# Down projection of a decoder layer: four chunks of features, the middle two by seven block products

## The chip, the cores and the metric

The kernel runs on one core of a Trainium2 chip. A core has a matrix engine (TensorE, PE in the profile; its weight loads are PEld), a vector engine (VectorE, DVE), a scalar engine (ScalarE, ACT), GpSimd (POOL) and SyncE (SP), which issues most transfers. Work lies in SBUF (128 partitions), matmuls accumulate in banks of PSUM, and transfers between device memory and SBUF go through 16 DMA engines. The metric is device time in microseconds (us) of one execution of the whole program.

## The reference, cut to what matters

One layer of a hybrid decoder over 576 tokens (512 of a prompt, 64 of samples), width 1024: a mixer, a cross attention, and at the end a gated feed-forward with 2816 hidden features. The change lies in the last part:

```python
u = _rms(x) * g_pre_ffn
f = (jax.nn.silu(u @ w_gate) * (u @ w_up)) @ w_down
x = x + _rms(f) * g_post_ffn
```

## The kernel before

All large products are made in split form. A float32 operand is kept as a high part (rounded to the matmul type `float32r`) and a low part (the remainder), and a product takes three matmuls: high by high, high by low, low by high. So every weight that is loaded must be split: ACT casts the high part (`whi`), and the low part (`wlo`, `wacc`) is made by a subtraction on DVE, or by ACT writing the negated high part and a POOL transfer accumulating the weight onto it (`accum_op=ALU.add`).

The 2816 hidden features are 22 blocks of 128; gate and up weights have one unit of 1024 columns per feature block (8 blocks of inputs by 128). Tokens are 576 columns, in halves of 288 (`EHALVES`) or of 256 and 320 (`HALVES`).

Feature blocks 0 to 3 are made plainly, in a stretch whose order is written out by hand: `at_(p, ...)` puts each step at a place p of a plan, and the plan is issued in that order. Blocks 4 to 21 are made by the class `Pair` (L1659). It takes two neighbouring feature blocks j and j+1 as a 2 by 2 grid: inputs in two halves, tokens in two halves. Seven products of blocks take the place of eight (Winograd's form of Strassen's scheme). The weights' sums and differences are made on DVE in `sums` and `diffs`, and split in `parts2`, `parts3` and `parts4`; the sums of the token blocks were made once. One unit (the gate, or the up weights of one pair of blocks) has 7 products of 4 x 3 matmuls of 288 columns, 84 in all. `prepare` issues the preparation of a unit. Its matmuls come in three parts: `early` (products 0 and 1), `mid` (2, 3, 4) and `late` (5, 6), and `pairs` issues early, the previous unit's late, then mid. `done` (L1734) takes a result from PSUM: the gate passes through silu into the tile `gt`, the up product is multiplied onto it, and the hidden block is split into `hh` and `hl`.

The down projection is cut into three chunks of feature blocks: 0 to 7, 8 to 15 and 16 to 21 (the loop at L1846, and L1853 onward). In a chunk, `down_chunk` (L1794) makes all 8 output blocks in both halves, with 24 matmuls in the first two chunks (18 in the last) for each. Chunk 0 copies the results into the tile `f2` (`ev_first`, ACT), chunk 1 adds to it (`ev_add`, DVE), and the last chunk adds and goes on to the norm. Pairs 4 and 6 come before chunk 0, pairs 8 to 14 before chunk 1, pairs 16 to 20 before the last one.

What sets the order: outside the hand-written stretches a planner reorders the instructions of each engine before the run, by its own estimate of when operands and buffers are ready; on the chip each engine works through its queue in the order given. Buffers come from small rings: raw weights `raw` (2) and `rawx` (2), `whi` (3), `wlo` (3), `wacc` (2), and three PSUM banks for each of two sides. A load on SP waits for its raw buffer, and all later loads of SP wait behind it.

Of the kernel before, what the change touches and what calls it, by code (L numbers as in the profile page):

```python
# [11 lines left out]
F32 = mybir.dt.float32  # L12
# [3 lines left out]
ALU = mybir.AluOpType  # L16
# [100 lines left out]
def build(nc, tc, ctx, I, O):  # L117
# [912 lines left out]

    ph = ctx.enter_context(tc.tile_pool(name="rows", bufs=1, reuse_waits="tile"))
    spb.close()
# [386 lines left out]

    u3h = SL(3, "u3h", F32R)  # L1420
    u3l = SL(5, "u3l", F32R)
# [217 lines left out]
    def lows(n_, src):  # L1639
        hi, lo = parts(n_)  # L1640
        V.tensor_tensor(lo, src, hi.bitcast(F32), op=ALU.subtract)

    b11, b21, b22 = [[t_[:, 4 * k:4 * k + 4, c] for t_ in (u3h, u3l)] for k, c in ((0, E[0]), (1, E[0]), (1, E[1]))]
    for p, out, a, b in ((17.1, B11, B12, B11), (17.5, B12, B22, B12), (17.95, B22, B22, B11), (18.4, B21, B21, B22)):
# [8 lines left out]

    LA, LB = slice(0, 512), slice(512, 1024)

    def K3(t_):
        return t_.rearrange("p (k c) -> p k c", c=P)

    class Pair:  # L1659

        def __init__(s, j, up, hh, hl):
            s.j, s.up, s.hh, s.hl = j, up, hh, hl
            s.src = I["wup" if up else "wgate"]
            s.r1 = wp.tile([P, 1024], F32, name="raw", tag="raw", bufs=2)
            S.dma_start(s.r1, s.src[j])

        def load(s):

            s.h4, s.ls = [t_[:, 0:4, 288 + P * s.up:416 + P * s.up] for t_ in (u3h, u3l)]
            s.r2 = fp.tile([P, 1024], F32, name="rawx", tag="rawx", bufs=2)  # L1670
            S.dma_start(s.r2, s.src[s.j + 1])
            s.l1 = fp.tile([P, 1024], F32R, name="wacc", tag="wacc", bufs=2)
            s.low(s.l1, s.r1, s.j)

        def low(s, out, raw, j, c=slice(0, 1024)):

            if ("gu"[s.up], j) in PRE:
                G.dma_start(out, pre[:, PRE.index(("gu"[s.up], j)), c])
            else:
                A.activation(out, raw, AF.Copy, scale=-1.0)  # L1680
                G.dma_start(out, s.src[j, :, c], accum_op=ALU.add)  # L1681

        def high1(s):
            s.h1 = wp.tile([P, 1024], F32R, name="whi", tag="whi", bufs=3)
            A.copy(s.h1, s.r1)

        def sums(s):
            V.tensor_tensor(sw[:, LB], s.r2[:, LA], s.r2[:, LB], op=ALU.add)
            V.tensor_tensor(sw[:, LA], sw[:, LB], s.r1[:, LA], op=ALU.subtract)

        def parts2(s):
            s.h2, s.l2 = [wp.tile([P, 1024], F32R, name=k, tag=k, bufs=3) for k in ("whi", "wlo")]
            split(s.h2, s.l2, sw)

        def diffs(s):
            V.tensor_tensor(s.r2[:, LA], s.r1[:, LA], s.r2[:, LA], op=ALU.subtract)
            V.tensor_tensor(s.r1[:, LB], s.r1[:, LB], sw[:, LA], op=ALU.subtract)

        def place3(s):
            s.h3, s.l3 = [wp.tile([P, 1024], F32R, name=k, tag=k, bufs=3) for k in ("whi", "wlo")]  # L1700
            s.low(s.l3[:, LA], s.r2[:, LB], s.j + 1, LB)

        def parts3(s):
            A.copy(s.h3, s.r2)
            V.tensor_tensor(s.ls, K3(s.r2[:, LA]), K3(s.h3[:, LA]).bitcast(F32), op=ALU.subtract)

        def parts4(s):
            split(s.h4, K3(s.l3[:, LB]), K3(s.r1[:, LB]))

        def factor(s, w):  # L1710

            if w == 6:
                return s.h4, K3(s.l3[:, LB])
            t_ = [getattr(s, k + "123"[w // 2]) for k in "hl"]
            c = LB if w % 2 else LA
            return K3(t_[0][:, c]), s.ls if w == 4 else K3(t_[1][:, LA if w == 5 else c])

# [4 lines left out]
        def bank(s):  # L1722
            return (MP if s.up else GP)("ps_u" if s.up else "ps_g")[:, :288]

        def mul(s, ps, w, b, start=True):
            fh, fl = s.factor(w)
            for k in range(4):
                wh, wl = fh[:, k, :], fl[:, k, :]
                mm(ps, wh, b[0][:, k, :], start=start and k == 0, stop=False, skip_group_check=True)  # L1729
                mm(ps, wh, b[1][:, k, :], start=False, stop=False, skip_group_check=True)  # L1730
                m = mm(ps, wl, b[0][:, k, :], start=False, stop=k == 3, skip_group_check=True)  # L1731
            return m

        def done(s, a, i, ps, more=None):  # L1734

            g = gates(s.j)[a][i]
            if not s.up:
                if more is not None:
                    V.tensor_tensor(g, ps, more, op=ALU.add)
# [7 lines left out]
            k = (s.j + a) % 8  # L1747
            split(s.hh[:, k, E[i]], s.hl[:, k, E[i]], g)

# [8 lines left out]
        def mid(s):  # L1758
            s.mul(s.x, 2, parts(2), False)
            s.c2, c3 = ct[:, 0, :], cc[:, 288:576]  # L1760
            s.ev2 = A.copy(s.c2, s.x)  # L1761
            s.z = s.bank()
            s.mul(s.z, 3, parts(1))
            s.mul(s.x, 4, parts(3), False)
# [9 lines left out]
    def pairs(js, hh, hl, last=None):  # L1774

        for j in js:
            for up in range(2):
                if last and j == 4:
                    continue
                with tc.issue_after((pp[1].ev2 if up else pp[0].ev3).ins) if j == 6 else ExitStack():  # L1780
                    p = Pair(j, up, hh, hl)
                    p.prepare()
                p.early()
                if last:
                    last.late()
                p.mid()
                last = p
        return last

    def down_part(c, nk, j, i, ps, w, k0, k1):  # L1790
        t0, n = HALVES[i]
        return gemm(ps, [(*w, nk)], act(hh), act(hl), t0, n, k0, k1)

    def down_chunk(c, nk, order, last, w_of, evac):  # L1794

        ps, n1 = {}, nk - 2

# [5 lines left out]
        for n_, (j, i) in enumerate(order[:3]):  # L1803
            down_part(c, nk, j, i, get(j, i), w_of(j), 0, n1)
            if n_ == 0:
                last.late()
        for n_, (j, i) in enumerate(order):
            p = get(j, i)
            m = down_part(c, nk, j, i, p, w_of(j), n1 if n_ < 3 else 0, nk)
            evac(n_, j, i, p, m)  # L1810
# [4 lines left out]

    def ev_add(n_, j, i, ps, m):
        t0, n = HALVES[i]
        V.tensor_tensor(f2[:, j, t0:t0 + n], f2[:, j, t0:t0 + n], ps, op=ALU.add)


    pp = []
    for n_ in range(2):
        at_(14.0 + n_ / 10, lambda n_: pp.append(Pair(4, n_, *H)), n_)
    for p, n_, step in ((19.05, 0, "load"), (19.1, 1, "load"), (21.9, 0, "sums"), (22.05, 0, "high1"), (22.6, 0, "diffs"),
# [6 lines left out]
    with tc.manual_schedule(engines={TE.engine, A.engine, V.engine, G.engine, S.engine}):  # L1831
# [6 lines left out]
        sw = fp.tile([P, 1024], F32, name="sw")  # L1838
        cc = rb_tile("cc")
        for p, _, fn in plan:  # L1840
# [69 lines left out]
    def half0(j, k):  # L1910
        if k == 0:
            tail[j] = (MP if j % 2 else GP)("ps_dn")[:, :256]
        down_part(2, 6, j, 0, tail[j], w_of(j), k, k + 1)

# [101 lines left out]
def pack(inp):  # L2016
# [37 lines left out]
    out["wup"] = _units(i["w_up"][0], KT)  # L2054
    out["wdown"] = _units(i["w_down"][0], NFFN)
    cs = i["state_conv"][0].reshape(NB, 3, 12, P)[:, :, order]
# [45 lines left out]
```

## Time and profile before

| | us |
|---|---|
| median of 3 runs | 1115.01 |
| lowest and highest run | 1114.74, 1115.77 |
| the profiled execution | 1114.63 |
| span in its profile (first to last instruction) | 1112.9 |
| PE busy in the span | 1097.6 (99%) |
| DVE busy | 707.3 (64%) |
| ACT busy | 591.1 (53%) |
| POOL busy | 213.3 (19%) |

In the profile, a row of a timeline gives the start, the length, the engine, the line of the code, the operation, and the tile written from the tiles read; in brackets stands the idle time of the engine ahead of it and what ended it. Matmuls overlap, so their lengths add up to more than the time they take, and the distance between their starts is what they cost. A group's row gives the number of instructions, their busy time, the mean length, and the idle time before them with its releaser.

### The profile page before, as it was taken

The numbers are of one execution on the slowest core, as the hardware profiler recorded it, in microseconds if no ns is written. First come the engines' busy times: TensorE is split into PE (matmuls) and PEld (weight loads), VectorE is DVE, ScalarE is ACT, GpSimd is POOL, SyncE is SP. The second block draws the span as 40 slices with busy tenths as digits, with TensorE's granted clock in tenths as the row PEclk, the third lists the DMA queues.
The fourth block names the chain that finished last, engine by engine and source line by source line (L and its number), as shares of the span: only waits on it lengthen the run. The fifth ranks groups of instructions, "written<-read, shape, count | busy, mean of one in ns | idle before, by whom it ended". The sixth has DMA issues, their size and how long they took to land.

```text
span 1112.9 us, 21074 instructions
## 1 busy us (share of the span) xinstructions
PE 1097.6 (99%) x8427; PEld 1050.7 (94%) x8427; DVE 707.3 (64%) x1391; ACT 591.1 (53%) x1068; POOL 213.3 (19%) x289
## 2 busy tenths in 40 slices
PE   9999999999999999999999999999999999999997
PEld 8999878998999999999988889999999999999997
DVE  6796776558877765569654455676533765447555
ACT  6877523246654555656454445556435674246654
POOL 1333544222222112000254301101001110011000
PEclk9999999999999999999999999999999999999999
DMA  6685544335745348552567765745535674257532
GB/s 210 162 164 129 152 133 161 124 90 150 216 136 148 81 152 290 197 195 93 191 224 252 284 209 167 249 114 124 142 95 123 167 174 126 86 123 171 120 136 86
DMA packets 55078, 176.57 MB, mean 159 GB/s; under 512 B 6044, under 2 KB 10268, under 8 KB 54468
## 3 DMA queue, kind: packets, MB, share of 16 engines
q1 hardware_dynamic: 41444, 137.47, 37.4%
q0 software_dynamic: 13248, 37.23, 16.6%
q8 instruction: 66, 1.08, 0.4%
q10 hardware_dynamic: 288, 0.52, 0.1%
q14 instruction: 32, 0.26, 0.1%
HBM read 154.54 MB, written 20.65 MB: 157 GB/s over the span
## 4 chain that ended last, share of the span: by engine, by line
PE 92%; DMA 2%; DVE 2%; ACT 2%; issue 1%; SPq 0%; DVEq 0%; ACTq 0%
PE ps_in L201 6%; PE ps_in L202 6%; PE ps_in L203 6%; PE ps_dn L201 4%; PE ps_dn L203 4%; PE ps_dn L202 4%; PE ps_o L201 3%; PE ps_o L203 3%; PE ps_o L202 3%; PE ps_g L1729 3%; PE ps_g L1730 3%; PE ps_g L1731 3%; PE ps_u L1729 3%; PE ps_u L1730 3%; PE ps_u L1731 3%; PE ps_v L778 2%
## 5 line engine op out<-in xcount | busy, mean ns | idle before, releaser
L181 ACT CAST whi<-raw 128x1024 fp32r<-128x1024 f32 x110 | 114.6, 1045 | 119.7 <-PE ps_in L202 26.1
L201 PE MATMUL ps_in<-uh,whi 128*128 128x320 f32 (+1 forms) x544 | 163.6, 301 | 0.0
L203 PE MATMUL ps_in<-uh,wlo 128*128 128x320 f32 (+1 forms) x544 | 163.2, 300 | 0.0
L202 PE MATMUL ps_in<-ul,whi 128*128 128x320 f32 (+1 forms) x544 | 162.6, 299 | 0.0
L188 DVE TENSOR_TENSOR wlo<-raw,whi 128x1024 fp32r<-128x1024 f32 (+1 forms) x102 | 107.4, 1055 | 81.3 <-ACT whi L181 80.4
L201 PEld LDWEIGHTS ps_in<-uh,whi 128*128 128x128 f32 x544 | 103.1, 190 | 2.4 <-issue 1.7
L203 PEld LDWEIGHTS ps_in<-uh,wlo 128*128 128x128 f32 x544 | 103.0, 190 | 1.2 <-issue 0.4
L202 PEld LDWEIGHTS ps_in<-ul,whi 128*128 128x128 f32 x544 | 103.2, 190 | 0.6
L201 PE MATMUL ps_dn<-hh,whi 128*128 128x320 f32 (+1 forms) x280 | 82.6, 298 | 0.5 <-ACT whi L181 0.5
L203 PE MATMUL ps_dn<-hh,wlo 128*128 128x320 f32 (+1 forms) x280 | 81.8, 294 | 0.8 <-DVE wlo L188 0.8
L202 PE MATMUL ps_dn<-hl,whi 128*128 128x320 f32 (+1 forms) x280 | 82.1, 294 | 0.0
L203 PEld LDWEIGHTS ps_dn<-hh,wlo 128*128 128x128 f32 x280 | 52.7, 189 | 1.2 <-DVE wlo L188 1.2
L201 PEld LDWEIGHTS ps_dn<-hh,whi 128*128 128x128 f32 x280 | 52.2, 188 | 1.0 <-ACT whi L181 0.7
L202 PEld LDWEIGHTS ps_dn<-hl,whi 128*128 128x128 f32 x280 | 52.8, 188 | 0.0
L186 POOL DMA_DIRECT2D wlo<-win x32 | 27.9, 881 | 89.2 <-ACT wlo L185 80.8
L1729 PE MATMUL ps_u<-b,whi 128*128 128x288 f32 x144 | 42.5, 295 | 0.6 <-ACT ct L1761 0.6
L1730 PE MATMUL ps_u<-b,whi 128*128 128x288 f32 x144 | 42.5, 296 | 0.0
L1729 PE MATMUL ps_g<-b,whi 128*128 128x288 f32 x144 | 42.5, 295 | 0.0
L1730 PE MATMUL ps_g<-b,whi 128*128 128x288 f32 x144 | 42.5, 295 | 0.0
L201 PE MATMUL ps_o<-mixs_h,whi 128*128 128x320 f32 (+1 forms) x128 | 38.3, 299 | 1.1 <-ACT f_mix L1014 1.1
L201 PE MATMUL ps_xo<-qh,whi 128*128 128x288 f32 x128 | 37.8, 301 | 1.0 <-ACT f_xo L1417 1.0
L1681 POOL DMA_DIRECT2D wacc<-wgate x9 | 7.8, 872 | 161.3 <-ACT wacc L1680 141.2
(728 smaller groups left out, 3664.6 us busy)
## 6 DMA issues: line engine op xcount, KB each, us to landing
raw<-win SPq DMA_DIRECT2D x35, 512.0 KB, 3.8
raw<-wout SPq DMA_DIRECT2D x17, 512.0 KB, 3.8
kva<-kc SPq DMA_DIRECT2D x16, 512.0 KB, 7.1
kva<-vc SPq DMA_DIRECT2D x16, 512.0 KB, 6.4
raw<-wdown SPq DMA_DIRECT2D x16, 512.0 KB, 3.5
raw<-wxq SPq DMA_DIRECT2D x13, 512.0 KB, 3.6
raw<-wgate SPq DMA_DIRECT2D x13, 512.0 KB, 3.6
raw<-wup SPq DMA_DIRECT2D x13, 512.0 KB, 5.1
```

Source lines behind the costliest of these rows:

```text
L181: A.copy(hi[:, :n], raw[:, :n])
L186: G.dma_start(lo[:, a:b], src[:, a:b], accum_op=ALU.add)
L188: e.tensor_tensor(lo[:, a:b], raw[:, a:b], hi[:, a:b].bitcast(F32), op=ALU.subtract)
L201: mm(ps, wh, ah, start=i == 0, stop=False)
L202: mm(ps, wh, al, start=False, stop=False)
L203: m = mm(ps, wl, ah, start=False, stop=i == len(tiles) - 1)
L778: m = mm(o, ah, lo[:, j:j + 256], start=False, stop=k == KT - 1, skip_group_check=True)
L1681: G.dma_start(out, s.src[j, :, c], accum_op=ALU.add)
L1729: mm(ps, wh, b[0][:, k, :], start=start and k == 0, stop=False, skip_group_check=True)
L1730: mm(ps, wh, b[1][:, k, :], start=False, stop=False, skip_group_check=True)
L1731: m = mm(ps, wl, b[0][:, k, :], start=False, stop=k == 3, skip_group_check=True)
```

## The change

The down projection gets four chunks: blocks 0 to 3, 4 to 9, 10 to 15 and 16 to 21. The first and the last stay plain. The middle two are made like the gate and up weights: a class `Down` shares the base class `Seven` with `Pair`, takes two output blocks by two groups of three feature blocks by two halves of tokens, and makes 7 products of 3 x 3 matmuls of 288 columns (63), four units to a chunk. Its weight units have 768 columns. Each product that an output needs is added to `f2` by DVE (`add`, seven additions a unit).

The right-hand side is now the hidden activations, so their block sums must be made for each chunk. `Hidden` holds a chunk's hidden blocks and sums in split form; its `sums` makes the four sums in the place of the gates (the tile `gt`) once both halves of a pair of blocks are there, and splits them in one go. Three of the four blocks of a pair are split by themselves, the fourth is only needed in sums. The host lays out the feature blocks of `w_down` so that the first of each pair form one group and the second the other. Storage: sums and blocks lie in `hh` and `hl`, in a new tile `te`, and in the unused end of the slot that holds `u3h`; the pool of rows moves to the right side of SBUF, is closed, and makes room for the pool with `te` and `cc`; it is opened again after the third chunk.

The order: chunk 0 follows pair 4 directly; then pairs 6 and 8, the gate unit of pair 10, four Down units, the up unit of pair 10, pairs 12 and 14, the gate unit of pair 16, four Down units, the up unit of pair 16, pairs 18 and 20, the last chunk. A unit's matmuls are issued as before: early, the previous unit's late, mid.

```diff
-    ph = ctx.enter_context(tc.tile_pool(name="rows", bufs=1, reuse_waits="tile"))
+    phs = ExitStack()
+    ph = phs.enter_context(tc.tile_pool(name="rows", bufs=1, side="right", reuse_waits="tile"))
...
-    u3h = SL(3, "u3h", F32R)
+    u3_ = SL(3, "u3h", F32R, (P, 5120))
+    u3h = u3_[:, 0:KT * T].rearrange("p (k t) -> p k t", t=T)
...
-    class Pair:
+    class Seven:
+        def weights_of(s, src1, src2, side, low=(None, None)):
+            s.n, s.side, s.src1, s.src2, s.made = src1.shape[-1] // 2, side, src1, src2, low
+            s.LA, s.LB, s.all = slice(0, s.n), slice(s.n, 2 * s.n), slice(0, 2 * s.n)
             s.r1 = wp.tile([P, 1024], F32, name="raw", tag="raw", bufs=2)
-            S.dma_start(s.r1, s.src[j])
+            S.dma_start(s.r1[:, s.all], src1)
...
+    class Pair(Seven):
...
         def late(s):
-            s.mul(s.x, 5, parts(4), False)
+            s.mul(s.x, 5, tsum[4], False)
             s.done(1, 0, s.x)
             s.mul(s.z, 6, b22, False)
             s.done(0, 1, s.z, s.c2)
+            if s.then:
+                s.then()
...
+    class Hidden:
...
+        def put(s, j, a, i, g):
+            if (a, i) != (0, 1):
+                split(*s.place((j - 4) // 2 % 3, {(0, 0): 4, (1, 0): 5, (1, 1): 6}[a, i]), g)
+
+        def sums(s, j):
+            q, g = (j - 4) // 2 % 3, gates(j)
+            for out, p, m in ((g[0][0], g[0][1], g[0][0]), (g[0][1], g[1][1], g[0][1]), (g[1][1], g[1][1], g[0][0]),
+                              (g[1][0], g[1][0], g[1][1])):
+                V.tensor_tensor(out, p, m, op=ALU.subtract)
+            hi, lo = [t_[:, (8, 0)[q]:(8, 0)[q] + 4, :] for t_ in s.b] if q < 2 else [s.rest()[:, 0:4, :], s.rest()[:, 4:8, :]]
+            split(hi, lo, gt[:, 4 * (j // 2 % 2):4 * (j // 2 % 2) + 4, :])
...
+    class Down(Seven):
+        def __init__(s, j, k0, hid):
+            s.j, s.hid, s.name = j, hid, "dn"
+            s.weights_of(I["wdown"][j, :, k0:k0 + 768], I["wdown"][j + 1, :, k0:k0 + 768], 1 - j // 2 % 2)
+
+        def add(s, a, i, ps):
+            o = f2[:, s.j + a, E[i]]
+            V.tensor_tensor(o, o, ps, op=ALU.add)
+
+        def early(s):
+            s.x, s.z, y = s.bank(), s.bank(), s.bank()
+            s.mul(s.x, 0, s.hid.block(4))
+            s.add(0, 0, s.x)
+            s.mul(s.z, 3, s.hid.block(0))
+            s.add(1, 1, s.z)
+            s.mul(y, 1, s.hid.block(5))
+            s.add(0, 0, y)
+            s.mul(s.x, 2, s.hid.block(3), False)
+            s.add(0, 1, s.x)
+
+        def mid(s):
+            s.mul(s.x, 4, s.hid.block(1), False)
+            s.add(1, 1, s.x)
+
+        def late(s):
+            s.mul(s.x, 5, s.hid.block(2), False)
+            s.add(1, 0, s.x)
+            s.mul(s.z, 6, s.hid.block(6), False)
+            s.add(0, 1, s.z)
...
-    for c, (js, ev) in enumerate((((4, 6), ev_first), ((8, 10, 12, 14), ev_add))):
-        if c:
-            hh, hl = SL0("hh%d" % c), SL(2, "hl%d" % c, F32R)
-        last = pairs(js, hh, hl, None if c else pp[1])
-        w_of = lambda j: weights(("d", j, c), I["wdown"][j, :, 1024 * c:1024 * c + 1024], cut=1024)
-        down_chunk(c, 8, [(j, i) for j in range(8) for i in (1, 0)], last, w_of, ev)
-    hh, hl = SL0("hh2"), SL(2, "hl2", F32R)
-    last = pairs((16, 18, 20), hh, hl)
+    def w_first(j):
+        with tc.issue_after(pp[0].ev3.ins) if j < 2 else ExitStack():
+            return weights(("d", j), I["wdown"][j, :, 0:512], 512, cut=512)
+    down_chunk(4, [(j, i) for j in range(8) for i in (1, 0)], pp[1], w_first, ev_first, 4)
+    last = run([pair(j, up, stores[0]) for j in (6, 8) for up in range(2)], None)
...
+    for n_, j0 in enumerate((10, 16)):
+        store = stores[-1]
+        last = run([lambda: Pair(j0, 0, None)] + downs(512 + 768 * n_, store), last)
+        stores.append((Plain if n_ else Hidden)(SL0("hh%d" % n_), SL(2, "hl%d" % n_, F32R)))
+        last = run([pair(j0, 1, stores[-1])] + [pair(j, up, stores[-1]) for j in (j0 + 2, j0 + 4) for up in range(2)], last)
+    hh, hl = stores[-1].b
+    tps.close()
+    ph = ctx.enter_context(tc.tile_pool(name="rows2", bufs=1, side="right", reuse_waits="tile"))
...
-    down_chunk(2, 6, [(j, 1) for j in (6, 7, 0, 1, 2, 3, 4, 5)], last, w_of, down_evac)
+    down_chunk(6, [(j, 1) for j in (6, 7, 0, 1, 2, 3, 4, 5)], last, w_of, down_evac, 4)
```

More of the change, by code (lines that the diff above doesn't have):

```diff
@@ L1640, in lows @@
         hi, lo = parts(n_)
+        tsum[n_] = [[t_[:, m, :] for m in range(4)] for t_ in (hi, lo)]
         V.tensor_tensor(lo, src, hi.bitcast(F32), op=ALU.subtract)
-    b11, b21, b22 = [[t_[:, 4 * k:4 * k + 4, c] for t_ in (u3h, u3l)] for k, c in ((0, E[0]), (1, E[0]), (1, E[1]))]
+    b11, b21, b22 = [[[t_[:, 4 * k + m, c] for m in range(4)] for t_ in (u3h, u3l)]
+                     for k, c in ((0, E[0]), (1, E[0]), (1, E[1]))]
+    tsum = {}
     for p, out, a, b in ((17.1, B11, B12, B11), (17.5, B12, B22, B12), (17.95, B22, B22, B11), (18.4, B21, B21, B22)):
@@ L1672, in load, with low @@
             s.l1 = fp.tile([P, 1024], F32R, name="wacc", tag="wacc", bufs=2)
[L1673 to L1678, printed above, removed]
+            s.low(s.l1[:, s.all], s.r1[:, s.all], s.src1, s.made[0])
+        def low(s, out, raw, src, made):
+            if made is not None:
+                G.dma_start(out, made)
             else:
                 A.activation(out, raw, AF.Copy, scale=-1.0)
-                G.dma_start(out, s.src[j, :, c], accum_op=ALU.add)
+                G.dma_start(out, src, accum_op=ALU.add)
@@ L1722, in bank, with __init__ @@
         def bank(s):
-            return (MP if s.up else GP)("ps_u" if s.up else "ps_g")[:, :288]
+            return (MP if s.side else GP)("ps_" + s.name)[:, :288]
         def mul(s, ps, w, b, start=True):
             fh, fl = s.factor(w)
-            for k in range(4):
+            nk = s.n // P
+            for k in range(nk):
                 wh, wl = fh[:, k, :], fl[:, k, :]
-                mm(ps, wh, b[0][:, k, :], start=start and k == 0, stop=False, skip_group_check=True)
-                mm(ps, wh, b[1][:, k, :], start=False, stop=False, skip_group_check=True)
-                m = mm(ps, wl, b[0][:, k, :], start=False, stop=k == 3, skip_group_check=True)
-            return m
+                mm(ps, wh, b[0][k], start=start and k == 0, stop=False, skip_group_check=True)
+                mm(ps, wh, b[1][k], start=False, stop=False, skip_group_check=True)
+                m = mm(ps, wl, b[0][k], start=False, stop=k == nk - 1, skip_group_check=True)
+            return m
+    class Pair(Seven):
+        def __init__(s, j, up, put, then=None):
+            s.j, s.up, s.put, s.then, s.name = j, up, put, then, "gu"[up]
+            src = I["wup" if up else "wgate"]
+            low = [pre[:, PRE.index((s.name, k)), c] if (s.name, k) in PRE else None
+                   for k, c in ((j, slice(0, 1024)), (j + 1, slice(512, 1024)))]
+            s.weights_of(src[j], src[j + 1], up, low)
         def done(s, a, i, ps, more=None):
@@ L1772, in late @@
             s.done(0, 1, s.z, s.c2)
[L1774 to L1787, printed above, removed]
-        return last
@@ L1790, in down_part, with __init__, rest, place @@
-    def down_part(c, nk, j, i, ps, w, k0, k1):
+            if s.then:
+                s.then()
+    class Hidden:
+        def __init__(s, hh, hl):
+            s.b = [t_.rearrange("p k (i t) -> p (k i) t", i=2) for t_ in (hh, hl)]
+            s.te = None
+        def rest(s):
+            if s.te is None:
+                s.te = tp.tile([P, 9, 288], F32R, name="te", tag="te")
+            return s.te
+        def place(s, q, m):
+            if q < 2:
+                return [t_[:, (8, 0)[q] + m, :] for t_ in s.b]
+            if m in (4, 5):
+                return [t_[:, (7, 15)[m - 4], :] for t_ in s.b]
+            if m == 6:
+                return [s.rest()[:, 8, :], u3_[:, KT * T:KT * T + 288]]
+            return [s.rest()[:, m, :], s.rest()[:, 4 + m, :]]
+        def put(s, j, a, i, g):
[8 more added lines that the diff above has]
+            split(hi, lo, gt[:, 4 * (j // 2 % 2):4 * (j // 2 % 2) + 4, :])
+        def block(s, m):
+            return [[s.place(q, m)[e] for q in range(3)] for e in range(2)]
@@ new lines, in run, with pair, make @@
+    def run(make, last):
+        for m in make:
+            p = m()
+            p.prepare()
+            p.early()
+            if last:
+                last.late()
+            p.mid()
+            last = p
+        return last
+    def pair(j, up, store):
+        def make():
+            with tc.issue_after(pp[1].ev2.ins) if j == 6 and not up else ExitStack():
+                return Pair(j, up, store.put, (lambda: store.sums(j)) if up and isinstance(store, Hidden) else None)
+        return make
@@ L2054, in pack @@
     out["wup"] = _units(i["w_up"][0], KT)
-    out["wdown"] = _units(i["w_down"][0], NFFN)
+    w = _units(i["w_down"][0], NFFN)
+    taken = [0, 1, 2, 3] + [j + k for j in (4, 10) for k in (0, 2, 4, 1, 3, 5)] + list(range(16, 22))
+    out["wdown"] = np.ascontiguousarray(w.reshape(8, P, NFFN, P)[:, :, taken].reshape(w.shape))
     cs = i["state_conv"][0].reshape(NB, 3, 12, P)[:, :, order]
```

77 lines of the change are left out of this document (42 added, 35 removed).

## The prediction

> **What bounds the kernel now.** I read the page first: its shares, the granted clock, the chain.
>
> ```profile
> span 1112.9 us, 21074 instructions
> PE 1097.6 (99%) x8427; PEld 1050.7 (94%) x8427; DVE 707.3 (64%) x1391; ACT 591.1 (53%) x1068; POOL 213.3 (19%) x289
> ...
> PEclk9999999999999999999999999999999999999999
> ...
> PE 92%; DMA 2%; DVE 2%; ACT 2%; issue 1%; SPq 0%; DVEq 0%; ACTq 0%
> ```
>
> TensorE (PE) is busy in 99% of the span at the full granted clock, and 92% of the chain that ended last is its matmuls. Time goes only where matmuls go, or where a new wait appears on PE. The second view is what PE waited for from 760 us to the end, the stage that the change touches (the whole answer):
>
> ```profile
> PE ps_ss L1891 <- ACT sq L1920: 0.8, 1, 0.8
> PE ps_dn L203 <- DVE wlo L188: 0.8, 2, 0.6
> PE ps_u L1729 <- ACT ct L1761: 0.6, 1, 0.6
> PE ps_dn L201 <- ACT whi L181: 0.5, 1, 0.5
> ```
>
> That is 2.7 us in 350 us. The third view gives the engines' busy time in four stretches: the first plain down chunk, gate and up pairs, the second down chunk, and six pair units alone.
>
> ```profile
> 809.00:854.00 45.00, 44.78 (x339) 44.58 (x339) 14.81 (x18) 15.93 (x29) 2.59 (x3) 1.00 0.44 111
> 854.00:899.00 45.00, 45.00 (x343) 45.00 (x342) 29.15 (x50) 31.71 (x53) 6.92 (x8) 1.00 0.71 164
> 944.00:996.00 52.00, 51.39 (x388) 51.19 (x387) 23.47 (x39) 14.08 (x18) 2.59 (x3) 1.00 0.38 97
> 871.30:937.90 66.60, 66.60 (x506) 66.60 (x505) 45.95 (x82) 45.10 (x77) 8.04 (x10) 1.00 0.66 155
> ```
>
> The columns are stretch, sum, PE, PEld, DVE, ACT, POOL, clock, DMA share, GB/s. A plain down chunk leaves DVE and ACT mostly idle. Pair units, which already do seven block products for eight, load DVE and ACT to 69% and 68% (45.95 and 45.10 of 66.6), with PE never idle. The change turns much of the former into something like the latter.
>
> **The matmuls saved.** The mean duration of a matmul (some 0.29 us) is not its price, because matmuls overlap. The price is the distance between starts:
>
> ```profile
> 871.30 0.29 PE L1729 MATMUL ps_g<-u3h,whi 128*128 128x288 f32 x1
> 904.62 0.29 PE L1729 MATMUL ps_u<-u3h,whi 128*128 128x288 f32 x1
> 937.94 0.31 PE L201 MATMUL ps_dn<-hh,whi 128*128 128x320 f32 x1
> ...
> 962.71 0.31 PE L201 MATMUL ps_dn<-hh,whi 128*128 128x320 f32 x1
> 969.08 0.31 PE L201 MATMUL ps_dn<-hh,whi 128*128 128x320 f32 x1
> ```
>
> From 871.30 to 937.94 lie six pair units of 7 products x 4 blocks x 3 matmuls = 84, so 504 matmuls of 288 columns in 66.64 us: 0.1322 us each, 11.1 us a unit. From 962.71 to 969.08 lie the two halves of one output block in chunk 1: 48 matmuls (24 of 320 columns, 24 of 256) in 6.37 us, 0.1327 each.
>
> Of the 22 feature blocks of the down projection, 0 to 3 and 16 to 21 stay plain with equal counts. Blocks 4 to 15 cost 12 x 16 x 3 = 576 matmuls now: 576 x 0.1327 = 76.4 us. After, each of two chunks of six blocks runs 4 Down units of 7 x 3 x 3 = 63 matmuls: 504 in all, the count between the first two rows and the third, so 66.6 us. Saved: **9.8 us**.
>
> The Trainium skill ("TensorE: Matmul & The Clock Gate", section "Wait — 56ns, not 53.3ns?") gives warm starts N / 2.4 GHz + 2.5 ns apart, 122.5 ns for 288 columns; an estimate by that page is 72 x 0.1225 = 8.8 us saved. The rows are about 10 ns above it, so the sum goes by the rows.
>
> **The work added beside PE.** Distances between starts, from a busy stretch of the pairs:
>
> ```profile
> 871.87 1.22 DVE L193 TENSOR_TENSOR wlo<-sw,whi 128x1024 fp32r<-128x1024 f32 x1
> 873.00 0.68 DVE L193 TENSOR_TENSOR wlo<-raw,u3h 128x512 fp32r<-128x512 f32 x1
> 873.61 0.68 DVE L1688 TENSOR_TENSOR sw<-rawx 128x512 f32<-128x512 f32 x1
> ...
> 875.54 0.45 DVE L1739 TENSOR_TENSOR gt<-ps_g,cc 128x288 f32<-128x288 f32 x1
> 875.90 0.68 DVE L1705 TENSOR_TENSOR u3l<-rawx,whi 128x512 fp32r<-128x512 f32 x1
> ```
> ```profile
> 868.84 1.03 ACT L1685 CAST whi<-raw 128x1024 fp32r<-128x1024 f32 x1
> 869.77 0.63 ACT L1680 ACTIVATE wlo<-rawx 128x512 fp32r<-128x512 f32 x1
> 870.31 1.03 ACT L192 CAST whi<-sw 128x1024 fp32r<-128x1024 f32 x1
> ```
>
> DVE takes 1.13 us for 1024 columns, 0.61 for 512, 0.36 for 288 from PSUM; on that line 384 columns cost 0.48 and 768 cost 0.87. A Down unit gives DVE two weight sums, two differences and two subtractions of 384 columns (6 x 0.48), one of 768 (0.87) and seven additions to f2 (7 x 0.36): 6.3 us within the 63 x 0.1322 = 8.33 us that PE needs, 75%. ACT takes 0.93 and 0.54; four operations of 768 (0.73) and two of 384 (0.42) make 3.8 us, 45%. For the hidden blocks, six up units each gain four subtractions of 288 and one split of 1152 in place of one of 288: on DVE 4 x 0.36 + 1.26 - 0.36 = 2.3 us. A gate and an up unit together then load DVE at most 2 x 7.66 + 2.3 = 17.6 of 22.2 us, 79%. No engine passes PE, so this work costs nothing by its amount; its cover is the 20% left and the buffers' lead.
>
> DMA: a pair unit loads 2 x 512 KB and accumulates 512 + 256 KB in 11.1 us; a Down unit moves three quarters of that in three quarters of the time, the same rate, with rows a quarter shorter. From below the share of the 16 engines stays at 0.71; were the time per row fixed it would be 0.71 x 11.1 / 8.33 = 0.95. I take it near the lower end, since 512 KB and 384 KB loads differ in landing by about their bytes (rows below). POOL issues two more accumulating transfers per Down unit, 16 in all, about 0.87 us each of an engine 81% idle.
>
> **The lead of the weights.** The longest chain runs from the place of the fourth factor coming free (in u3's unused quarter) to low parts two units later:
>
> ```profile
> 853.85 0.29 PE L1729 MATMUL ps_g<-u3h,whi 128*128 128x288 f32 x1
> ...
> 882.47 0.62 ACT L192 CAST u3h<-raw 128x512 fp32r<-128x512 f32 x1 [0.20 <-PE ps_u L1730]
> 884.18 0.68 DVE L193 TENSOR_TENSOR wlo<-raw,u3h 128x512 fp32r<-128x512 f32 x1
> 888.43 1.06 ACT L1680 ACTIVATE wacc<-raw 128x1024 fp32r<-128x1024 f32 x1 [0.42 <-DMA raw<-wup]
> 889.79 0.86 POOL L1681 DMA_DIRECT2D wacc<-wup  x1 [7.70 <-ACT wacc L1680]
> ...
> 830.76 0.33 SPq L1665 DMA_DIRECT2D raw<-wgate  x1
> ```
> ```profile
> raw<-wdown SPq DMA_DIRECT2D x16, 512.0 KB, 3.5
> raw<-wgate SPq DMA_DIRECT2D x13, 512.0 KB, 3.6
> wacc<-wup POOLq DMA_DIRECT2D x9, 512.0 KB, 5.5
> raw<-wdown SPq DMA_DIRECT2D x4, 384.0 KB, 3.0
> ```
>
> The low parts land at 889.79 + 5.5 = 895.3, 12.8 us after 882.47, and are used at 904.62: 9.3 us early. In Down units the deadline shrinks to 9 + 126 matmuls, 17.8 us, the chain hardly: about 5 us early. I price it at 0.
>
> **Where a wait can appear.** (1) From the first chunk, now four blocks deep, to pair 6. The raw buffer of its first weights comes free when the split of output block 6 is done, and that waits for block 3's weight buffers. In the old chunk the load left at 830.76, 23.1 us before its end at 853.85, and block 3 had been done four blocks before the end, 4 x 6.37 = 25.5. Now four blocks are 12.8 us and the shorter split takes 0.9 less than 2.4, so the load leaves 11.3 us before the end; 3.6 load, 1.1 negation and 5.5 accumulation leave 1.1 us. With a load of 5 us it is late. From 0 to 1.5; taken: **0.5**. SP's next loads queue behind this one, with 48 matmuls (6.3 us) of the gate unit as cover.
>
> (2) At the first Down unit of each chunk the second product needs the block sums: an addition, a multiplication, four subtractions, ACT's cast of 1152 and the last subtraction, some 4.8 us with hand-overs, against 36 + 9 matmuls (5.9 us); the product of block 5 needs no sums and can go ahead. From 0 to 1.5; taken: **0.3** each, 0.6.
>
> (3) Inside each Down unit the third product in a bank waits for DVE to have read it: 18 matmuls (2.4 us) for an addition of 0.45 plus PE's 0.29 tail. The second factor's low part waits for a buffer that the previous unit's last product frees, with 20 matmuls (2.6 us) for 0.9 + 0.3. What queues behind those DVE instructions is the next unit's preparation. Between 0, as in the six pair units, and two waits of 0.6, the worst of this stage: 0 to 1.2 a unit; near the first row: **0.2**, times 8 is 1.6.
>
> (4) The rows pool moves to the other end of SBUF, closes for the sums and opens again, so other old tiles must be free first; the tiles at those points were last used in earlier stages. 0, within 1 us either way. The new hidden tile must wait for the last Down unit, which PE has queued directly behind the early part of the pair that fills it: 0.
>
> **Sum** against the profiled execution (1114.63 us; span 1112.9 and 1.73 around it; the median of the runs is 1115.01): 1114.63 - 9.8 + 0.5 + 0.6 + 1.6 = **1107.5 us**. With every wait at its upper end, 1.5 + 3.0 + 9.6, it is 1118.9; with none and 1 us from the layout, 1103.8.
>
> **Rivals.** *Partly eaten*: waits of about 0.7 us per Down unit, from hand-overs or from transfers late at a share nearer 0.95: 8 x 0.7 + 1.1 gives 1111.5. For it speaks the queue order of DVE, fixed before the run; against it, no such wait in 504 matmuls of the pairs. *Cancelled*: both waits of (3) come each time, 8 x 1.2 + 1.1: 1115.5.
>
> *Slower: DVE sets the pace.* In the pair stretch DVE is idle 20.65 us in six units, 3.4 a unit. If those gaps belong to the preparation chain and not to PE's pace, a Down unit takes 6.3 + 3.4 = 9.7 us, 11 us more in eight; if the pairs are at their limit too, the 2.3 us in six up units come on top, 14 us. With the 1.1 of (1) and (2) that gives 1116.9 to 1130.7, with a middle of 1124. It decides from 9.4 us a Down unit (8.33 + (9.8 - 1.1) / 8), or 3.1 us of DVE gaps. For it: over half of the gaps in that stretch, 12.5 us, end on an ACT cast:
>
> ```profile
> L193 DVE TENSOR_TENSOR hl<-gt,hh 128x288 fp32r<-128x288 f32 x12 | 5.4, 456 | 6.3 <-ACT hh L192 6.3
> L1697 DVE TENSOR_TENSOR raw<-raw,sw 128x512 f32<-128x512 f32 x5 | 3.5, 692 | 6.2 <-ACT whi L1685 6.2
> ```
>
> Against it: PE never waits beside them, and the casts themselves wait for PE to give buffers back, as the 0.20 in the row of 882.47 shows.
>
> *Weight loading, not matmul count, is the bound*: then still 72 loads fewer, the same saving; no separate case.
>
> **Chances.** 1103.8 to 1110.5: 0.60; partly eaten, 1110.5 to 1112.8: 0.14; cancelled, within 0.2% (about what a measurement of this kernel can tell from no change; 1112.8 to 1117.2): 0.08; slower: 0.18. So faster 0.74, same 0.08, slower 0.18. The range, 1103.8 to 1116.5, leaves out some of the slow case and a little below; the likeliest case has its own, 1103.8 to 1110.5.
>
> **What would show it.** PE with 72 matmuls fewer (8355); 63 matmuls of a Down unit in 8.3 to 8.5 us; DVE near 75% there; waits of PE on DVE additions to f2 or on wlo below 2 us in all; at most 1.5 us of wait at pair 6. Wrong would be Down units of 9.5 us or more, POOL's accumulations landing well above 5.5 us, or waits in the pair units on DVE.

## The result and the profile after

The change made the kernel slower: 1118.53 us median (1115.41 to 1120.24, 11 runs) against 1115.35 (1114.43 to 1116.38, 11 runs), ratio 1.0026 with a 95% interval of 1.0018 to 1.0034. The forecast was 1107.5 with a range up to 1116.5. Single executions of the changed kernel spread over 4.8 us, those of the kernel before over 2.0. The profiled execution took 1116.74 us, with a span of 1114.9; it is 1.8 us below the median, so what follows accounts for less than the median lost.

The page of the changed kernel, in the lines that answer to those of before:

```profile
span 1114.9 us, 21198 instructions
PE 1092.4 (98%) x8355; PEld 1044.4 (94%) x8355; DVE 754.8 (68%) x1503; ACT 613.3 (55%) x1108; POOL 227.5 (20%) x305
...
PE 85%; DMA 7%; ACT 3%; DVE 2%; issue 1%; SPq 0%; DVEq 0%; ACTq 0%
```

The 72 matmuls are gone (8427 to 8355). PE's busy time fell by 5.2 us only, where 9.8 had been forecast, and its idle time rose from 15.3 to 22.5 us (span less busy time): 7.2 - 5.2 = the 2.0 us by which the span grew. DMA, 2% of the chain that ended last before, is now 7% of it.

What PE waited for from 755 us on:

```profile
PE ps_g L1734 <- ACT whi L1688: 5.5, 2, 2.8
PE ps_dn L1735 <- DVE te L193: 1.0, 2, 0.5
PE ps_ss L1998 <- ACT sq L2027: 0.8, 1, 0.8
PE ps_dn L1734 <- DVE f_ffn L1833: 0.8, 2, 0.4
PE ps_u L1734 <- ACT whi L1688: 0.8, 1, 0.8
PE ps_g L1734 <- ACT cc L1778: 0.7, 1, 0.7
PE ps_u L1734 <- ACT cc L1778: 0.6, 1, 0.6
```

The large term is L1688, ACT's cast of a pair unit's first high part (`high1`): 6.3 us in three waits. All three lie where four Down units end and pair units begin again. The wait on L1998 belongs to the norm at the end and is as long in the kernel before. In the stretches below (columns as before: stretch, sum, PE, PEld, DVE, ACT, POOL, clock, DMA share, GB/s), the first is the Down units of the second chunk but for their two ends (213 of 252 matmuls), the second the pair units up to the first long wait, the third those up to the second one, the fourth what follows it:

```profile
864.70:894.38 29.68, 28.77 (x215) 28.23 (x213) 22.17 (x45) 13.77 (x21) 5.01 (x6) 1.00 0.68 160
894.38:904.84 10.46, 7.83 (x59) 7.59 (x58) 7.76 (x15) 5.71 (x9) 1.89 (x3) 0.99 0.74 175
1001.10:1012.73 11.63, 8.01 (x59) 7.54 (x57) 7.78 (x15) 6.73 (x11) 2.59 (x3) 1.00 0.70 161
1012.73:1058.80 46.07, 46.07 (x337) 46.07 (x338) 29.94 (x53) 28.99 (x50) 5.17 (x6) 0.96 0.63 139
```

In the Down stretch PE is idle for 0.9 of 29.68 us, and DVE is busy in 75% of it. The loss comes behind it. The timeline at the first long wait, SP's loads first, then ACT, DVE and PE:

```profile
887.10 0.33 SPq L1668 DMA_DIRECT2D raw<-wgate  x1
897.69 0.33 SPq L1668 DMA_DIRECT2D raw<-wup  x1
...
883.65 0.82 ACT L1688 CAST whi<-raw 128x768 fp32r<-128x768 f32 x1
892.33 1.06 ACT L1683 ACTIVATE wacc<-raw 128x1024 fp32r<-128x1024 f32 x1 [2.70 <-DMA raw<-wgate]
893.30 1.03 ACT L1688 CAST whi<-raw 128x1024 fp32r<-128x1024 f32 x1
902.47 1.06 ACT L1683 ACTIVATE wacc<-raw 128x1024 fp32r<-128x1024 f32 x1 [3.65 <-DMA raw<-wup]
903.43 0.41 ACT L192 CAST hh<-gt 128x288 fp32r<-128x288 f32 x1
903.75 1.04 ACT L1688 CAST whi<-raw 128x1024 fp32r<-128x1024 f32 x1
...
896.98 0.69 DVE L193 TENSOR_TENSOR wlo<-raw,u3h 128x512 fp32r<-128x512 f32 x1
...
901.92 0.29 PE L1736 MATMUL ps_u<-b,wlo 128*128 128x288 f32 x1
904.84 0.61 PE L1734 MATMUL ps_g<-u3h,whi 128*128 128x288 f32 x1 [2.63 <-ACT whi L1688]
905.24 0.44 PE L1735 MATMUL ps_g<-u3l,whi 128*128 128x288 f32 x1
905.48 0.44 PE L1736 MATMUL ps_g<-u3h,wacc 128*128 128x288 f32 x1
```

PE ran dry at 902.2 and needed the cast at 903.75, whose operand had been in SBUF since the load before (issued at 887.10, used by ACT at 892.33). ACT stood idle for 3.65 us until 902.47, because the instruction at the head of its queue was a negation (L1683) for the unit *after* the next one, and that one's raw weights (issued at 897.69) had not landed. The cast stood behind it.

It is a loop. The cast of one unit releases the difference, the fourth factor and its low part, which free the raw buffer (896.98); SP then issues a load (897.69); it takes about 4.8 us (902.47); its negation stands ahead of the next unit's cast (903.75). From cast to cast the chain takes 10.45 us (893.30 to 903.75), and 9.65 from 883.65 to 893.30. PE consumes a pair unit in 11.1 us and a Down unit in 8.3. So the loop is mostly hidden while pairs follow pairs, and shows where Down units run into pairs. At the first long wait it can be read off: the cast of 893.30 came just in time for the matmul of 894.38, PE then had 7.83 us of matmuls in its queue (second stretch), and the turn took 10.45; the difference is the wait of 2.63.

The 1.3 us of waits on ACT's copies (L1778) have the same cause. Each of these two copies stands directly behind a negation that had waited for its load, 3.10 us at 818.00 and 2.64 at 935.91. They lie among pair units, one of them ahead of the first Down unit, so a late load can cost time there too.

Behind the wait the matmuls start 0.24 us apart instead of 0.13: the clock is down (0.96 in the last stretch as a mean). Starts from 905.24 on cost 1.3 us more than at 0.13, those behind the second long wait about 1.5. With the first matmul after each wait that is some 3 us of the missing 4.6 in PE's busy time; the rest of it I have not located.

### The profile page after: what moved, and what is told of

Read it like the earlier page. It is cut to its first block, busy times and chain, and to the rows that moved or that the text cites. A ratio compares the mean times of both kernels' runs of the same rounds, so it can differ in the third digit from the quotient of the medians.

```text
span 1114.9 us, 21198 instructions
## 1 busy us (share of the span) xinstructions
PE 1092.4 (98%) x8355; PEld 1044.4 (94%) x8355; DVE 754.8 (68%) x1503; ACT 613.3 (55%) x1108; POOL 227.5 (20%) x305
## 3 DMA queue, kind: packets, MB, share of 16 engines
q8 instruction: 65, 1.06, 0.4%
## 4 chain that ended last, share of the span: by engine, by line
PE 85%; DMA 7%; ACT 3%; DVE 2%; issue 1%; SPq 0%; DVEq 0%; ACTq 0%
PE ps_in L201 6%; PE ps_in L202 6%; PE ps_in L203 6%; PE ps_o L201 3%; PE ps_o L203 3%; PE ps_o L202 3%; PE ps_g L1734 3%; PE ps_g L1735 2%; PE ps_g L1736 2%; PE ps_u L1734 2%; DMA raw<-wgate 2%; PE ps_u L1735 2%; PE ps_u L1736 2%; PE ps_v L778 2%; PE ps_v L777 2%; PE ps_v L776 2%
## 5 line engine op out<-in xcount | busy, mean ns | idle before, releaser
L181 ACT CAST whi<-raw 128x1024 fp32r<-128x1024 f32 (+1 forms) x102 | 102.9, 1012 | 94.1 <-PE ps_in L202 26.1
L188 DVE TENSOR_TENSOR wlo<-raw,whi 128x512 fp32r<-128x512 f32 (+1 forms) x94 | 93.6, 996 | 67.5 <-ACT whi L181 66.3
L1707 ACT CAST whi<-rawx 128x1024 fp32r<-128x1024 f32 (+1 forms) x26 | 25.6, 986 | 36.0 <-PE ps_dn L1735 23.3
L1683 ACT ACTIVATE wacc<-raw 128x1024 fp32r<-128x1024 f32 (+1 forms) x26 | 25.7, 993 | 31.8 <-DMA raw<-wup 14.3
L201 PE MATMUL ps_xq<-u2h,whi 128*128 128x320 f32 (+1 forms) x128 | 38.3, 303 | 0.0
L203 PE MATMUL ps_o<-mixm_h,wlo 128*128 128x256 f32 (+1 forms) x128 | 38.2, 298 | 0.0
L202 PE MATMUL ps_xq<-u2l,whi 128*128 128x320 f32 (+1 forms) x128 | 38.0, 299 | 0.0
L202 PE MATMUL ps_o<-mixm_l,whi 128*128 128x256 f32 (+1 forms) x128 | 38.0, 297 | 0.0
L203 PE MATMUL ps_xq<-u2h,wlo 128*128 128x320 f32 (+1 forms) x128 | 37.9, 297 | 0.0
```

The costliest lines, as they stand in the source:

```text
L181: A.copy(hi[:, :n], raw[:, :n])
L188: e.tensor_tensor(lo[:, a:b], raw[:, a:b], hi[:, a:b].bitcast(F32), op=ALU.subtract)
L201: mm(ps, wh, ah, start=i == 0, stop=False)
L202: mm(ps, wh, al, start=False, stop=False)
L203: m = mm(ps, wl, ah, start=False, stop=i == len(tiles) - 1)
L1707: A.copy(s.h3[:, s.all], s.r2[:, s.all])
```

## The experiments

The theory: **ACT's queue**, a negation that waits for a raw load ahead of a cast that PE needs. The rivals: **late transfers** (two raw buffers and a busier DMA are the limit, whatever the order), and **DVE** as the pace of the Down units (the slower rival of the prediction). Two more questions were the slow clock and which of the units lose the time. The kernel before ran again beside the experiments (medians 1114.99 to 1115.73 us); the changed kernel did not, so a difference to its 1118.53 is uncertain by some tenths of a us beyond the intervals given.

**1. The order in ACT's queue.** One dependency is added in every unit from pair 6 on: the negation is issued behind the previous unit's cast.

```diff
-            s.low(s.l1[:, s.all], s.r1[:, s.all], s.src1, s.made[0])
+            with tc.issue_after(h1s[-1].ins) if len(h1s) > 1 else ExitStack(): s.low(s.l1[:, s.all], s.r1[:, s.all], s.src1, s.made[0])
...
-            A.copy(s.h1[:, s.all], s.r1[:, s.all])
+            h1s.append(A.copy(s.h1[:, s.all], s.r1[:, s.all]))
```

> Edit: in every unit from pair 6 on, ACT's negation for the low part of the first factor is ordered behind the previous unit's cast of its first high part; nothing else changes. Queue theory (the negation waits for a raw load at the head of ACT's queue, and the cast that PE needs stands behind it): the waits of PE on that cast, 6.3 us in the changed kernel, fall below 1 us, the slow matmuls behind them (about 2.6 us) go too, and the time falls by 7 to 10 us, to about 1108 to 1111, faster than the kernel before. Rival, the transfers are late as such (two raw buffers, a busier DMA): the load lands as late as now, PE then waits for the accumulated low part instead, and the time changes by less than 2 us. Rival, DVE sets the pace of the Down units: less than 2 us as well.

Measured: 1109.84 us (1108.26 to 1112.23), ratio to the kernel before 0.9949 (0.9935 to 0.9963). Beside the changed kernel's 1118.53 that is 8.7 us. The edit states one dependency per unit; the planner, which then orders the queues anew, may have moved other instructions with it, and the waits on the sums in `te` grew from 1.0 to 2.3 us. The reordered kernel's waits from 755 us on:

```profile
PE ps_dn L1735 <- DVE te L193: 2.3, 2, 1.2
PE ps_ss L1998 <- ACT sq L2027: 0.8, 1, 0.8
PE ps_u L1734 <- ACT ct L1774: 0.7, 2, 0.4
PE ps_dn L1734 <- DVE f_ffn L1833: 0.6, 2, 0.3
```

No wait on L1688 is left, and the mean granted clock is 1.000. On its ACT timeline the negation still waits for its load, 2.93 us, but behind the cast:

```profile
899.69 1.05 ACT L1688 CAST whi<-raw 128x1024 fp32r<-128x1024 f32 x1
900.65 0.62 ACT L1683 ACTIVATE wlo<-rawx 128x512 fp32r<-128x512 f32 x1
904.20 1.06 ACT L1683 ACTIVATE wacc<-raw 128x1024 fp32r<-128x1024 f32 x1 [2.93 <-DMA raw<-wup]
```

The loads did not get faster. Median time from issue to landing of the gate units' raw weights in the changed and in the reordered kernel:

```profile
raw<-wgate SPq DMA_DIRECT2D x13, 512.0 KB, 4.8
```
```profile
raw<-wgate SPq DMA_DIRECT2D x13, 512.0 KB, 5.4
```

So slow transfers by themselves are out: with loads that take longer the kernel is 8.7 us faster.

**2. The negation on POOL.**

```diff
-                A.activation(out, raw, AF.Copy, scale=-1.0)
+                G.tensor_scalar(out, raw, -1.0, None, op0=ALU.mult)
```

> Edit: the negation runs on POOL ahead of its accumulating transfer, in every unit; ACT no longer waits for any raw load. Queue theory: as in the run with the other order, 1108 to 1112, if POOL's negation of 1024 columns stays below about 3 us; POOL was idle four fifths of the span. Late-transfer rival: PE waits for low parts, less than 2 us of change. DVE rival: no gain, or a loss, since POOL then reads SBUF beside DVE.

Measured: 1113.39 us (1111.30 to 1115.71), ratio 0.9977 (0.9965 to 0.9989). The gain has the expected sign, 5.1 us beside the changed kernel, but is 1.4 us short of the expected range. PE's two largest waits, and the group of POOL's negations:

```profile
PE ps_g L1736 <- DMA wacc<-wgate: 3.2, 1, 3.2
PE ps_dn L1734 <- DVE f_ffn L1833: 1.2, 2, 0.8
```
```profile
L1683 POOL TENSOR_SCALAR wacc<-raw 128x1024 fp32r<-128x1024 f32 (+1 forms) x24 | 65.7, 2736 | 116.5 <-DMA raw<-wgate 50.9 <-DMA raw<-wdown 27.7 <-DMA raw<-wup 16.0
```

The group's mean mixes two widths. For 1024 columns alone POOL takes 2.96 us on average, just inside the condition of 3 us, where ACT takes 1.06. Now the low part itself is late once, by 3.2 us, at the gate unit of pair 6, the first one behind the first chunk.

**3 and 4. The slow clock.** A control pins the matmul order around the two long waits. The second kernel is the control with 20 matmuls into an unused bank in each of the two waits; their results are not used.

```diff
...
+                ps = B0("ps_fill")
+                with tc.issue_after(last.m3.ins):
+                    for _ in range(20):
+                        mf = mm(ps[:, 0:288], u3h[:, 0, 0:P], u3h[:, 0, 0:288], start=True, stop=True, skip_group_check=True)
+                with tc.issue_after((mf if 20 else last.m3).ins):
+                    m1 = p.early()
+                with tc.issue_after(m1.ins):
+                    last.rest()
...
```

> Control for the next run: the matmul order around the two long waits is pinned (waits, then the 24 matmuls of the next gate unit's early part, then the up unit's product 4). Expected within 1.5 us of the changed kernel, two waits of 2 to 3 us, starts 0.24 us apart for some 3 us behind each, mean granted clock about 0.996.

> Edit: the control with 20 unused matmuls of 288 columns (2.6 us) put into each of the two long waits of PE. If the slow matmuls behind the waits come from PE's idleness, the granted clock stays at 1.00, starts are 0.13 us apart from the first, and the kernel with 40 more matmuls is 2 to 3 us faster than the control. If the slow clock has another cause, the time is the same, or up to 1 us longer.

Measured: the control 1117.31 us (1115.71 to 1120.23), with the filling 1119.87 (1119.46 to 1121.04), ratios 1.0016 (1.0005 to 1.0027) and 1.0039 (1.0024 to 1.0053). The forecast of 2 to 3 us of gain failed, and a loss of 2.6 us lies outside the other case as well. One reason is in the control: it kept to its time, but only the first of the two filled places had a long wait, 2.58 us with slow starts behind it. At the second PE waited 1.12 us, less than 20 matmuls take. The timeline of the filled kernel at the first place:

```profile
903.89 2.79 PE L1872 MATMUL ps_fill<-u3h 128*128 128x288 f32 x20
906.68 0.40 PE L1734 MATMUL ps_g<-u3h,whi 128*128 128x288 f32 x1
906.92 0.30 PE L1735 MATMUL ps_g<-u3l,whi 128*128 128x288 f32 x1
907.05 0.29 PE L1736 MATMUL ps_g<-u3h,wacc 128*128 128x288 f32 x1
```

At this place the idle time and the slow starts are both gone: 0.13 us apart from the second matmul on. But PE then ran into ACT's queue one unit later. Its waits on the cast fell from 6.7 us in the control to 0.6, while those on ACT's copy of product 4 (L1785 in both, L1778 in the changed kernel) rose from 0.8 to 5.9, of which 4.6 on the up units. One of these is 2.7 long with slow starts behind it, and on ACT's timeline the copy for it stands directly behind a negation that waits for its load:

```profile
PE ps_u L1734 <- ACT cc L1785: 4.6, 2, 2.7
```
```profile
915.87 1.06 ACT L1683 ACTIVATE wacc<-raw 128x1024 fp32r<-128x1024 f32 x1 [4.75 <-DMA raw<-wgate]
...
917.16 0.38 ACT L1785 COPY cc<-ps_u 128x288 f32<-128x288 f32 x1
```

So time won on PE is not kept while ACT's queue sets the pace. The slow starts go with PE's idleness in this pair of runs, at one place each; what they cost in all was not isolated.

**5. The same order in the kernel before.**

> Edit: the same reordering (negation behind the previous unit's cast) in the kernel before the change. Queue theory with the loop of 9.7 to 10.5 us a unit: pair units take PE 11.1 us, so the loop is hidden there and nothing is gained: within 0.2% of the kernel before, 1113 to 1117. If the order cost time in any unit, also in pairs, this kernel is 3 us or more faster than before.

Measured: 1115.41 us against 1115.47, ratio 0.9998 (0.9989 to 1.0007). The order costs nothing that these runs can tell where only pair units follow each other. It became a cost with the change.

**6. More work on DVE.** On top of experiment 1, into a tile that nothing reads there:

```diff
+            for j in range(3):
+                V.tensor_tensor(cc[:, 0:288], f2[:, s.j, E[1]], f2[:, s.j, E[0]], op=ALU.add)
```

> Edit, on top of the reordered kernel (1109.8): three more additions of 288 columns on DVE in every Down unit, into a tile that nothing reads (about 1.1 us of DVE work a unit, 8.7 us in eight). If DVE set the pace of the Down units, 7 to 9 us slower than the reordered kernel. Queue theory: DVE has the room, less than 3 us slower.

Measured: 1110.43 us, ratio 0.9959 (0.9945 to 0.9973), beside 0.9949 (0.9935 to 0.9963) without: no difference that these runs tell, and not the 7 to 9 us of a kernel that DVE paces. The same stretch of Down units, without and with the extra work:

```profile
864.64:895.20 30.56, 29.00 (x215) 28.30 (x214) 23.50 (x47) 14.37 (x22) 5.23 (x6) 1.00 0.68 166
```
```profile
864.64:895.20 30.56, 28.99 (x215) 28.25 (x214) 27.09 (x57) 13.62 (x21) 4.68 (x6) 1.00 0.67 158
```

DVE goes from 77% to 89% busy (23.50 and 27.09 of 30.56), and PE's work in the stretch stays the same. DVE is not the pace.

**7. The order of products in a Down unit.** On top of experiment 1, product 1 comes ahead of product 3:

```diff
-            s.mul(s.z, 3, s.hid.block(0))
-            s.add(1, 1, s.z)
             s.mul(y, 1, s.hid.block(5))
             s.add(0, 0, y)
+            s.mul(s.z, 3, s.hid.block(0))
+            s.add(1, 1, s.z)
```

> Edit, on top of the reordered kernel: a Down unit makes product 1 ahead of product 3, so that the first product that needs block sums comes 9 matmuls (1.2 us) later. The two waits of 1.2 us on the sums in te fall below 0.3 us; 1 to 3 us faster than the reordered kernel, 1107 to 1109.

Measured: 1105.56 us (1104.69 to 1109.31), ratio 0.9912 (0.9894 to 0.9929). The waits from 755 us on are nearly all gone:

```profile
PE ps_ss L1998 <- ACT sq L2027: 0.8, 1, 0.8
PE ps_dn L1735 <- DVE te L193: 0.7, 2, 0.4
PE ps_u L1734 <- ACT ct L1774: 0.4, 1, 0.4
```

It is 4.3 us faster than experiment 1. The two waits on `te` fell to 0.35 us each, not below the expected 0.3, and the time is 1.4 us below the expected range. The span of the profiled execution is 3.5 us shorter than in experiment 1 (1104.0 against 1107.5). Of these, the waits on `te` account for 1.6, those on `f2` for 0.6 and those on `ct` for 0.3; PE's busy time is 1.0 lower (1088.1 against 1089.1). Why the waits on `f2` went too was not looked into. The median is 9.9 us below the kernel before (about 8 to 12 by the interval), near the whole of the matmuls' saving, and the best of the versions run.

**8. No negation in Down units.** On the changed kernel's own order, the low part of a Down unit's first factor is a subtraction on DVE:

```diff
-            s.low(s.l1[:, s.all], s.r1[:, s.all], s.src1, s.made[0])
+            s.low(s.l1[:, s.all], s.r1[:, s.all], s.src1, s.made[0]) if s.name != "dn" else None
...
             A.copy(s.h1[:, s.all], s.r1[:, s.all])
+            if s.name == "dn":
+                V.tensor_tensor(s.l1[:, s.all], s.r1[:, s.all], s.h1[:, s.all].bitcast(F32), op=ALU.subtract)
```

> Edit, on top of the changed kernel with its own order: in Down units the low part of the first factor is made by one subtraction of 768 columns on DVE, so there is no negation and no accumulation for it. Queue theory: the loop is opened in four units of each chunk, so the lead of the loads is kept; the negations of the pair units behind the Down units still stand ahead of the casts. The waits on the cast fall by more than half, 1110 to 1114. If DVE sets the pace, 0.9 us more a unit: 1122 or more.

Measured: 1116.85 us (1114.29 to 1121.61), ratio 1.0007 (0.9994 to 1.0020). A miss, by 2.9 us: I had held that lead is lost unit by unit through the Down units. The waits on the cast did not go. They are read here from the slowest of ten executions (1121.61 us), so their size at the median is not known:

```profile
PE ps_g L1736 <- ACT whi L1688: 5.5, 2, 3.1
...
PE ps_u L1736 <- ACT whi L1688: 0.9, 2, 0.5
```

**9 and 10. Where the order matters.** The first has the dependency only at the negations of the gate and up units of pairs 12 and 18, the second everywhere but there.

```diff
-            with tc.issue_after(h1s[-1].ins) if len(h1s) > 1 else ExitStack(): ...
+            with tc.issue_after(h1s[-1].ins) if s.name != "dn" and s.j in (12, 18) else ExitStack(): ...
```

> Edit: the reordering at four places only, the negations of the gate and up units of pairs 12 and 18, which are two units ahead of the casts at which PE waited; everywhere else the changed kernel's own order. If the loss sits where PE was seen to wait, all of the reordered kernel's gain is kept: 1108 to 1112, no wait of PE on the cast. If the Down units themselves lose lead step by step in the loop, half of it at most: 1113 to 1116.

> Edit: the complement, the reordering at every unit but those four. If the loss sits at the four places: within 2 us of the changed kernel, 1116 to 1120, with waits of PE on the cast of some 5 us in all. If the loop through the Down units loses the lead: 1110 to 1114.

Measured: the four places 1113.60 us (1111.13 to 1115.77), ratio 0.9983 (0.9973 to 0.9993); the rest 1120.65 (1117.20 to 1122.43), ratio 1.0055 (1.0039 to 1.0072). PE's largest waits with the four places, and the largest three with the rest (this profile is of its fastest execution, 1117.20):

```profile
PE ps_g L1734 <- ACT cc L1778: 3.6, 3, 1.6
PE ps_u L1734 <- ACT whi L1688: 1.2, 2, 0.7
```
```profile
PE ps_g L1734 <- ACT whi L1688: 4.5, 2, 2.2
PE ps_dn L1735 <- DVE te L193: 2.3, 2, 1.2
PE ps_u L1734 <- ACT whi L1688: 2.2, 2, 1.4
```

The rest alone gains nothing: the waits on the cast stay (6.7 us), and the time is 2.1 us above the changed kernel and 0.7 above the range expected for this case. The four places alone take the waits on the cast from 6.3 to 1.2 us, but waits on ACT's copies out of PSUM (L1778) grow from 1.3 to 3.6, and 4.9 of the 8.7 us come back. That is not the whole gain that I expected of them: the time lies in the range that I had given to the other case, the loss in the Down units, which the run with the rest speaks against. So the four places are necessary, and not enough. Once they are cured, PE waits for copies that stand behind other negations (one at 1028.64, directly behind a negation that waited 3.08 us for its load), and the order elsewhere is worth the remaining 3.8 us (experiment 1 against the four places); without them it is worth nothing.

A third raw buffer, which would take the load itself out of the loop, was not tested.

## Why the prediction was wrong

*The matmuls saved: 9.8 us.* Right. The count fell by 72. In the changed kernel's Down units 183 matmuls without a wait (870.13 to 894.24) start 0.1325 us apart, where 0.1322 had been taken, and in experiment 7 PE's busy time is 9.5 us below the kernel before (1088.1 against 1097.6).

*The work added beside PE.* Right: 75% of DVE in the Down units was forecast and 75% measured (22.17 of 29.68); experiment 6 shows room above it.

*The lead of the weights: "about 5 us early. I price it at 0."* This step failed. I followed the raw weights to the place where they are used, the accumulated low part, and found time enough. I did not ask what is queued behind the negation on ACT while it waits. The quoted rows held the wait: 888.43 waits for its load, `[0.42 <-DMA raw<-wup]`. The cast of the other unit stands two short instructions behind it on ACT, in a row that I did not quote:

```profile
890.46 1.05 ACT L1685 CAST whi<-raw 128x1024 fp32r<-128x1024 f32 x1 [0.29 <-PE ps_u L1730]
```

There the wait did no harm, because the cast then still waited 0.29 us for PE. I also compared the chain with a deadline two units away, when it closes on itself after one: 9.7 to 10.5 us from cast to cast, against 11.1 for a pair unit and 8.3 for a Down unit. The 0 was 6.3 us of waits on the cast, 1.3 on the copies, and about 3 us of slow starts behind them: 10.6. Less the 0.9 by which the other waits came out below the sum (next paragraph) that is 9.7 us, where the profiled execution lies 9.2 above the forecast. The rest is small and open on both sides: 1.6 us of PE's busy time that I have not located, against 1.9 us of waits in the kernel before that the changed one no longer has.

*Where a wait can appear.* (1) Pair 6: 0.5 taken, no wait seen; the 3.2 us with the negation on POOL (experiment 2) fell there. (2) The sums: 0.6 taken, 1.0 measured. (3) Inside the Down units: 1.6 taken, 0.8 measured on `f2` (`f_ffn` in the profile). (4) The layout: 0 taken, none seen. Together 1.8 measured of the 2.7 taken.

*The rivals.* The slower case had the right sign and the wrong mechanism: it named DVE, which experiment 6 excludes. Its row "idle before, until ACT's cast" was the trace's hint at ACT's queue, and I read it as a matter of DVE. A slower case through ACT was not among the rivals, so its share of the chances was too small and the range ended 2 us too low.

## What to carry to other kernels

Where work per unit shrinks, look for loops through buffers and in-order queues whose turn had been hidden by the old unit's length: add up one turn, from an instruction over the buffer that it frees, the load, and the first consumer of that load, to whatever stands behind this consumer in its queue. An instruction that waits for a transfer belongs behind the instructions that another engine needs sooner; here that one order was worth 8.7 us, and nothing in the kernel before, where each unit takes PE 11.1 us and a turn as measured here 9.7 to 10.5. A lead that is long enough for the data says nothing on the engine that waits for it.

## What the runs showed of the hardware

I had not counted on the clock. In the changed kernel 2.63 us without matmuls were followed by starts 0.24 us apart for about 2.6 us, and 2.84 us by the same for about 3.3, beginning 1.2 us after the restart. In the other profiled executions, from 745 us on, idle stretches of 1.77, 2.21, 2.32, 2.58, 2.72 and 3.14 us were followed by such starts; stretches of 1.91, 2.25 and 3.23 us were not, nor was any of 1.57 us or less. So the length alone does not decide it; what else does was not isolated. The Trainium skill ("TensorE: Matmul & The Clock Gate", section "HAM oscillation — how this bites in real kernels") warns of idle gaps above some 3.4 us; these runs show starts at about half the rate after shorter ones, though not after each. With its slow starts the first long wait, 2.63 us, cost some 3.9.
